# Input projections by seven products of quarters, all ahead of the attention, with their results kept in DRAM

## The chip, the cores and the metric

The kernel runs on one core of a Trainium2 chip. The metric is the device time of one launch in microseconds. TensorE (PE) multiplies, VectorE (DVE), ScalarE (ACT) and GpSimd (POOL) do the elementwise work, and SyncE (SP) issues nearly all DMAs, one after the other in the order of its queue.

## The reference

One step of a hybrid decoder layer. 560 tokens (16 meta, 512 prompt, 32 sample tokens of 8 sequences) of width 1024 go through an RMS norm, and one wide projection feeds two branches:

```python
hn = rmsnorm(x, norm_g)
proj = jnp.einsum('btd,dn->btn', hn, w_in)
a_pool, z_pool, q, k, v, o, z_m, i_pre, f_pre, g_pool, g_mlstm = split_projection(proj)
y_pool = multiscale_pool(pool_buf, a_pool, ...) * silu(z_pool)      # trailing means, then a map per group
(C_new, n_new, m_new), h = mlstm_scan(q, k, v, ig, lf, state, ...)   # 4 heads of 512, matrix memory
y_mlstm = sigmoid(o) * layernorm_per_head(h) * silu(z_m)
u = sigmoid(g_pool) * (y_pool @ w_branch_pool) + sigmoid(g_mlstm) * (y_mlstm @ w_branch_mlstm)
y = rmsnorm(x + u @ w_out, final_g)
```

a_pool, z_pool, g_pool and g_mlstm are 1024 wide, q, k, v, o and z_m 2048 each. Besides y the outputs are the new states, among them the matrix memory of 8 sequences and 4 heads (512 x 512 each), which is read, scaled, added to and written.

## The kernel before

All products keep float32 accuracy with three passes: each operand is split into a high and a low part (`split`, L105: ACT casts the high part, DVE or POOL subtracts), and `mm3` (L123, its matmul is L129) multiplies low by high, high by low and high by high, for each of the 8 slabs of 128 inputs. The normed input lies in SBUF transposed, as `hT_hi` and `hT_lo` of 128 x 8 x 560.

A projection (`project`, L131) takes 128 columns of `w_in`: `weights` (L114) loads 512 KB in one DMA, ACT casts `whi`, DVE subtracts `wlo`, and 2 x 24 matmuls of 272 or 280 token columns fill two PSUM banks, which ACT or DVE read at once. V is made the other way round, with tokens on the partitions (L607, 512 columns).

The program is written in one order and a scheduler keeps dependences; each engine runs its own list strictly in that order. `begin` (L187) makes `hT` and the first two projections (L77); `gates` (L338) makes the rows of input and forget gates on 4 partitions and writes them to DRAM as `rows_d` (L407); `pooling` (L437) holds the projections of the pooling branch, and its work and the gates' run side by side. Then come four `head`s (L579 on): V, then q and k, then the state products `prompt_C` (L709) and `sample_C` (L726 to L736), the scores, and o and z_m of the head between them, the numerators and the layer norm. In a head the projections stand between the steps that wait for DVE and ACT. `final` (L955 on) does the branch products, `w_out` and the last norm. Weights are loaded some units ahead: `wraw`, `whi` and `wlo` share 12 buffers of 4 KB a partition. At a head's start `bc`, the head's gate rows on all partitions, is loaded from `rows_d` (L584).

What each head needs of the projections is used where it is made: q, k, v, o and z_m never leave SBUF or PSUM.

## Time and profile before

| what | value |
|---|---|
| median of 3 runs | 1133.23 us (1133.14 to 1138.13) |
| span of the profiled execution | 1129.6 us |
| PE, DVE, ACT, POOL busy | 98%, 54%, 33%, 19% of the span |
| bytes moved by DMA | 177.18 MB, 157 GB/s |
| granted TensorE clock, mean | 0.997 |

The profile shows one execution and gives its span, from the first to the last instruction; its own time, with what lies around the span, is not listed, and the timed runs' median stands 3.6 us above the span. A matmul's shown duration overlaps the next one's, so a matmul's cost is read from the spacing in the chain and not from its own mean.

### The profile page before, as it was taken

The numbers are of one execution on the slowest core, as the hardware profiler recorded it, in microseconds if no ns is written. First come the engines' busy times: TensorE is split into PE (matmuls) and PEld (weight loads), VectorE is DVE, ScalarE is ACT, GpSimd is POOL, SyncE is SP. The second block draws the span as 40 slices with busy tenths as digits, with TensorE's granted clock in tenths as the row PEclk, the third lists the DMA queues.
The fourth block names the chain that finished last, engine by engine and source line by source line (L and its number), as shares of the span: only waits on it lengthen the run. The fifth ranks groups of instructions, "written<-read, shape, count | busy, mean of one in ns | idle before, by whom it ended". The sixth has DMA issues, their size and how long they took to land.

```text
span 1129.6 us, 19419 instructions
## 1 busy us (share of the span) xinstructions
PE 1112.0 (98%) x7938; PEld 1016.7 (90%) x7938; DVE 613.9 (54%) x954; ACT 373.6 (33%) x688; POOL 218.8 (19%) x367
## 2 busy tenths in 40 slices
PE   7999999999999999999999999999999989999997
PEld 6999999989879889979889979889978889999976
DVE  6786732224545755446655456556447465265633
ACT  5642342113222343232342232343222334342322
POOL 4223220003205003205003215003214001020000
PEclk9999999999999999999999999999999999999999
DMA  8432433434566744566654566754565754343512
GB/s 210 128 110 73 111 86 107 126 97 113 178 204 211 231 143 135 176 203 221 222 164 124 173 193 204 232 176 118 167 223 192 237 179 133 107 132 118 180 52 84
DMA packets 188176, 177.18 MB, mean 157 GB/s; under 512 B 12479, under 2 KB 137167, under 8 KB 187563
## 3 DMA queue, kind: packets, MB, share of 16 engines
q1 hardware_dynamic: 188087, 175.94, 50.9%
q8 instruction: 62, 1.02, 0.4%
q14 instruction: 27, 0.22, 0.1%
HBM read 127.80 MB, written 47.39 MB: 155 GB/s over the span
## 4 chain that ended last, share of the span: by engine, by line
PE 77%; DMA 9%; DVE 8%; issue 2%; ACT 1%; SPq 1%; POOL 0%; DVEq 0%; POOLq 0%; ACTq 0%
PE ps L129 57%; PE ps L607 8%; DMA wraw<-in_w_in_dram 6%; DVE C L733 3%; PE ps L709 3%; PE ps L726 2%; PE ps L795 1%; DMA out_dram<-C 1%; PE ps L609 1%; ACT whi L108 1%; DVE wlo L111 1%; DVE vc L767 1%; DMA x<-in_x_prompt_dram 1%; PE ps L695 1%; PE ps L732 1%
## 5 line engine op out<-in xcount | busy, mean ns | idle before, releaser
L129 PE MATMUL ps<-hT_hi,wlo 128*128 128x272 f32 (+1 forms) x1504 | 439.5, 292 | 0.3 <-DVE yp L493 0.3
L129 PE MATMUL ps<-hT_hi,whi 128*128 128x272 f32 (+1 forms) x1504 | 435.3, 289 | 0.0
L129 PE MATMUL ps<-hT_lo,whi 128*128 128x272 f32 (+1 forms) x1504 | 435.1, 289 | 0.0
L111 DVE TENSOR_TENSOR wlo<-wraw,whi 128x1024 fp32r<-128x1024 f32 x134 | 168.0, 1254 | 338.3 <-ACT whi L108 227.0
L129 PEld LDWEIGHTS ps<-hT_hi,wlo 128*128 128x128 f32 x1504 | 284.2, 189 | 15.1 <-issue 10.4
L129 PEld LDWEIGHTS ps<-hT_hi,whi 128*128 128x128 f32 x1504 | 284.7, 189 | 0.0
L129 PEld LDWEIGHTS ps<-hT_lo,whi 128*128 128x128 f32 x1504 | 283.8, 189 | 0.2
L108 ACT CAST whi<-wraw 128x1024 fp32r<-128x1024 f32 x134 | 140.6, 1049 | 393.7 <-DMA wraw<-in_w_in_dram 313.6
L733 DVE SCALAR_TENSOR_TENSOR C<-C,bc,ps 128x512 f32<-128x512 f32 x128 | 87.4, 739 | 6.6 <-PE ps L732 6.6
L129 PE MATMUL ps<-yh,whi 128*128 128x272 f32 x256 | 72.9, 288 | 0.0
L129 PE MATMUL ps<-yl,whi 128*128 128x272 f32 x256 | 72.8, 288 | 0.0
L129 PE MATMUL ps<-yh,wlo 128*128 128x272 f32 x256 | 70.5, 289 | 0.0
L111 POOL TENSOR_TENSOR vl<-v,vh 128x512 fp32r<-128x512 f32 x16 | 31.8, 2023 | 110.3 <-issue 84.5
L607 PE MATMUL ps<-whi,hT_lo 128*128 128x512 f32 x128 | 50.5, 395 | 0.0
L607 PE MATMUL ps<-whi,hT_hi 128*128 128x512 f32 x128 | 50.4, 393 | 0.0
L607 PE MATMUL ps<-wlo,hT_hi 128*128 128x512 f32 x128 | 50.2, 393 | 0.0
L129 PEld LDWEIGHTS ps<-yh,whi 128*128 128x128 f32 x256 | 48.2, 188 | 0.0
L129 PEld LDWEIGHTS ps<-yl,whi 128*128 128x128 f32 x256 | 48.2, 188 | 0.0
L129 PEld LDWEIGHTS ps<-yh,wlo 128*128 128x128 f32 x256 | 46.9, 188 | 0.0
L726 PE MATMUL ps<-C,qm 128*32 128x512 f32 x256 | 40.7, 603 | 0.0
L111 POOL TENSOR_TENSOR kl<-k,kh 128x560 fp32r<-128x560 f32 x16 | 22.3, 1396 | 90.2 <-DVE r_hi L673 77.3
L129 PE MATMUL ps<-ypl,whi 128*128 128x272 f32 x128 | 36.9, 288 | 0.0
(315 smaller groups left out, 1806.7 us busy)
## 6 DMA issues: line engine op xcount, KB each, us to landing
wraw<-in_w_in_dram SPq DMA_DIRECT2D x112, 512.0 KB
C<-in_state_C_dram SPq DMA_DIRECT2D x64, 512.0 KB
out_dram<-C SPq DMA_DIRECT2D x64, 512.0 KB
wraw<-in_w_branch_mlstm_dram SPq DMA_DIRECT2D x16, 512.0 KB
bc<-rows_d SPq DMA_DIRECT2D x4, 1256.0 KB
wraw<-in_w_branch_pool_dram SPq DMA_DIRECT2D x8, 512.0 KB
out_dram<-c SPq DMA_DIRECT2D x16, 256.0 KB
wraw<-in_w_out_dram SPq DMA_DIRECT2D x8, 512.0 KB
```

Of the source, the lines that this page charges most:

```text
L108: nc.scalar.copy(hi, src)
L111: (lo_on or nc.gpsimd).tensor_tensor(lo, src, hi.bitcast(F32), ALU.subtract)
L129: self.nc.tensor.matmul(out, s, m, start=(j == 0), stop=(j == len(seq) - 1))
L607: nc.tensor.matmul(pv[i], s, w[:, k2], start=(k == 0 and j == 0), stop=(k == 7 and j == 2))
L609: nc.tensor.matmul(pv[4][:112], self.hS[:, k], w[:, k2], start=(k == 0 and j == 0), stop=(k == 7 and j == 1))
L695: nc.tensor.transpose(ps[:, i * P:(i + 1) * P], kw[:, i * P:(i + 1) * P], self.ident)
L709: nc.tensor.matmul(pc, s[:, i], m[:, i], start=(i == 0 and j == 0), stop=False)
L726: nc.tensor.matmul(pqc[r:r + 32], self.qm[:, d, 32 * b:32 * b + 32], Cs[bb // 2][:, bb % 2], start=(d == 0 and g == 0), stop=(d == 3 and g ...
L732: nc.tensor.matmul(pu, kwst[r:r + 12, g], vst[r:r + 12, g], start=True, stop=True, tile_position=(r, 0))
L733: V.scalar_tensor_tensor(C, C, wintb[:, b, 3:4], pu, ALU.mult, ALU.add)
L767: V.scalar_tensor_tensor(t[:n], vh[:n, i].bitcast(F32), vs[:n, i:i + 1], vl[:n, i].bitcast(F32), ALU.subtract, ALU.add)
L795: nc.tensor.matmul(pb[:, o:o + mv.shape[-1] - m], s, mv[:, m:], start=(j == 0), stop=(j == last[True]))
```

## The change

Two column tiles of 128 are now made together (`quad`, L171 of the new file). The 1024 inputs are cut in two halves of 4 slabs, the 256 columns in two of 128, the 560 tokens in two of 280, and the eight products of quarters are replaced by seven, on sums and differences of quarters. Sums of the input, `Sa` to `Sd`, are made once in `begin`; sums of the weights are made in each `quad`. Three results are kept by ACT (`keep`), and DVE makes three of the four output quarters from them (`total`). A `quad` has 84 matmuls where two `project`s had 96. V and the first two tiles of the pooling input stay as they were. There are 47 quads, 36 of 272 columns and 11 of 280.

The token columns are in another order (`COLS`), so that the two halves are alike. All projections come first (`projections`), head by head, with the pooling branch and the sample states between the o and z_m quads; q, k, v, the gates' product `og`, the pooling branch's `yp` and `sg` and the samples' `qc` go to DRAM. `attention` then reads them back, head by head. `rows_d` is now written in eight pieces, and V's first part reads two small pieces of it back (`sw`).

Three places show the new order. The first is SP's queue after the gate rows. `rows_d` is the gates' DRAM scratch, `wraw` a projection's weights, `bc` and `sw` gate rows on all partitions. Before:

```order
L410 DMA out_dram<-gm_524 4x8x1
L115 DMA wraw_1207<-in_w_in_dram 128x8x128
L407 DMA rows_d<-rw 4x2512
L115 DMA wraw_1268<-in_w_in_dram 128x8x128
L584 DMA bc_2640<-rows_d 128x2512
L115 DMA wraw_1347<-in_w_in_dram 128x8x128
L586 DMA bc_2640<-in_c_sel_dram 32x48
L115 DMA wraw_1474<-in_w_in_dram 128x8x128
```

and now, where `wraw_598` holds the first weights of V of head 0:

```order
L545 DMA rows_d<-em_498 4x544
L545 DMA rows_d<-wi_497 4x32
L545 DMA rows_d<-ws_496 4x560
L751 DMA sw_595<-rows_d 128x32
L752 DMA sw_595<-rows_d 128x32
L751 DMA sw_2708<-rows_d 128x32
L754 DMA wraw_598<-in_w_in_dram 128x2x512
L752 DMA sw_2708<-rows_d 128x32
L754 DMA wraw_632<-in_w_in_dram 128x2x512
```

The load of the first weights after the gates now stands behind the eight pieces of `rows_d` and behind a read of them, where before one weight load stood right in front of the write and the others around it.

The second is PE in a projection, with the PSUM bank first (`ps_...`). Before, where the second half of the tokens follows the first:

```order
L129 MATMUL ps_826<-hT_hi,wlo_823 128x272
L129 MATMUL ps_826<-hT_lo,whi_822 128x272
L129 MATMUL ps_826<-hT_hi,whi_822 128x272
L129 MATMUL ps_851<-hT_hi,wlo_823 128x272
L129 MATMUL ps_851<-hT_lo,whi_822 128x272
L129 MATMUL ps_851<-hT_hi,whi_822 128x272
```

and now, at the end of a q quad of head 0 (`Sc` is one of the input's sums, `wblo` and `wbhi` weights' sums):

```order
L146 MATMUL ps_814<-Sc_hi,wblo_811 128x272
L146 MATMUL ps_814<-Sc_lo,wbhi_810 128x272
L146 MATMUL ps_814<-Sc_hi,wbhi_810 128x272
L146 MATMUL ps_814<-hT_hi,wblo_811 128x272
L146 MATMUL ps_814<-hT_lo,wbhi_810 128x272
L146 MATMUL ps_814<-hT_hi,wbhi_810 128x272
```

Before, the next product goes to another bank; now the last product of the quad adds to the bank that DVE has to read between the two.

The third is SP's queue at the start of a head. `vpt` takes copies of the head's v parts, made by ACT and POOL or DVE. Before, in head 0:

```order
L629 DMA vs_d_2889<-vh_2643 48x512 x2
L629 DMA vs_d_2889<-vl_2644 48x512
L636 DMA vpt<-vh_2643 16x512
L636 DMA vpt<-vl_2644 16x512
L632 DMA vst_2646<-vs_d_2889 12x1x512 x8
L636 DMA vpt<-vh_2643 16x512
L115 DMA wraw_3279<-in_w_in_dram 128x8x128
L722 DMA C_3377<-in_state_C_dram 128x2x512
```

and now in head 1, where `k_1682`, `k_1694`, `k_1710` are the first three slabs of k, `q_...` slabs of q and `og` the head before's gated outputs:

```order
L1030 DMA k_1682_9601<-k_d 128x560
L1102 DMA v_1681_9593<-qc_d 32x512
L1010 DMA vpt<-vh_9568 16x512 x2
L1010 DMA vpt<-vl_9569 16x512
L1103 DMA v_1681_9593<-v_1681_9593 48x512
L1023 DMA q_1691_9636<-q_d 128x544
L1030 DMA k_1694_9642<-k_d 128x560
L1023 DMA q_1703_9667<-q_d 128x544
L1030 DMA k_1710_9708<-k_d 128x560
L1064 DMA out_dram<-c_1709_9705 128x512
L1183 DMA y_d<-og_9281 128x544
```

Before, weights and states stood behind the copies into `vpt`; now the slabs of q and k of the same head do, and its last ones stand behind the stores of the head before.

The diff, cut to what the new order and the new product consist of:

```diff
...
+    def quad(self, src, lo, dst, scale=None, f21=None):
+        nc = self.nc
+        V, A = nc.vector, nc.scalar
+        n = HN - lo
+
+        def wide(n, pair):
+            return self.c(n, F32R, (2, 4, P)) if pair else self.c(n, F32R, (4, 256))
+
+        def narrow(n):
+            return self.r(n, F32R)[:, :512].rearrange("p (k n) -> p k n", k=4)
+        ra, rb = (self.c(s, shape=(4, 256)) for s in ("wa", "wb"))
+        nc.sync.dma_start(ra, src[:, 0:4])
+        nc.sync.dma_start(rb, src[:, 4:8])
+        b11, b12, b21, b22 = ra[:, :, :P], ra[:, :, P:], rb[:, :, :P], rb[:, :, P:]
+        ta, tb = (self.c(s, shape=(2, 4, P)) for s in ("ta", "tb"))
+        w11 = self.parts(b11, lambda s: narrow("w1" + s))
+        V.tensor_tensor(ta[:, 0], b11, b12, ALU.add)
+        V.tensor_tensor(ta[:, 1], ta[:, 0], b22, ALU.add)
+        wa = self.parts(ta, lambda s: wide("wa" + s, True))
+        V.tensor_tensor(tb[:, 0], b12, b22, ALU.add)
+        V.tensor_tensor(tb[:, 1], ta[:, 1], b21, ALU.add)
+        w2 = self.parts(rb, lambda s: wide("w2" + s, False))
+        wb = self.parts(tb, lambda s: wide("wb" + s, True))
+        hT, S = self.hT, self.S
+
+        def quarter(half, kh):
+            return [tuple(t[:, 4 * kh + k, HN * half + lo:HN * half + HN] for t in hT) for k in range(4)]
+
+        def combined(s):
+            return [tuple(t[:, k, lo:] for t in S[s]) for k in range(4)]
+
+        def product(ps, w, movs, first):
+            self.mm3(ps[:, :n], [(w[0][:, k], w[1][:, k]) for k in range(4)], movs, first=first, check=False)
+
+        def at(w, j):
+            return tuple(t[:, j] for t in w)
+
+        def cols(w, j):
+            return tuple(t[:, :, j * P:(j + 1) * P] for t in w)
+
+        def keep(ps, name):
+            t = self.t(name)[:, :n]
+            A.activation(t, ps[:, :n], AF.Copy, scale=1.0 if scale is None else scale)
+            return t
+
+        def view(ap, c0, c1, how):
+            ap = ap[:, c0:c1]
+            return how(ap) if how else ap
+
+
+        def total(which, ps, other, s_ps, s_other):
+            for out, c0, c1, how in dst[which]:
+                x, y = view(ps, c0, c1, how), view(other, c0, c1, how)
+                if scale is not None:
+                    V.scalar_tensor_tensor(out, x, s_ps * scale, y, ALU.mult, ALU.add if s_other > 0 else ALU.subtract)
+                elif s_ps < 0:
+                    V.tensor_tensor(out, y, x, ALU.subtract)
+                else:
+                    V.tensor_tensor(out, x, y, ALU.add if s_other > 0 else ALU.subtract)
+
+        pa, pe = self.ps(), self.ps()
+        product(pa, w11, quarter(0, 0), True)
+        p1 = keep(pa, "p1")
+        product(pe, at(wa, 0), combined("a"), True)
+        e = keep(pe, "e")
+        product(pa, at(wa, 1), combined("b"), False)
+        u = keep(pa, "u")
+        product(pe, cols(w2, 1), combined("d"), False)
+        total("12", pe, u, 1, -1)
+        px = self.ps()
+        product(px, cols(w2, 0), quarter(0, 1), True)
+        total("11", px, p1, 1, 1)
+        product(pa, at(wb, 0), combined("c"), False)
+        total("22", pa, e, -1, 1)
+        product(pa, at(wb, 1), quarter(1, 1), False)
+        for out, c0, c1, how in dst["21"]:
+            A.activation(out, view(pa, c0, c1, how), f21 or AF.Copy, scale=1.0 if scale is None else scale)
+
+
...
+            self.v_d = scratch("v_d", H, NT, HD + 1)
+            self.qc_d = scratch("qc_d", H, 32, HD)
+            with reused("combined", side="right") as self.sp, reused("hidden") as self.ip:
+                self.S = {s: [self.sp.tile([P, 4, HN], F32R, name=f"S{s}_{p}") for p in ("hi", "lo")] for s in "abcd"}
+                with reused("begin") as self.wp:
+                    self.begin()
+                with reused("work") as self.wp:
+                    self.projections()
+            with reused("branch", side="right") as self.bp:
+                with reused("heads") as self.hp:
+                    self.attention()
+            with reused("final") as self.fp:
                 self.final()
...
+
+        x = {}
+        for half in range(2):
+            for kh in range(2):
+                x[half, kh] = self.wp.tile([P, 4, HN], F32, name=f"x{half}{kh}")
+                hi, lo = (t[:, 4 * kh:4 * kh + 4, HN * half:HN * half + HN].bitcast(F32) for t in self.hT)
+                G.tensor_tensor(x[half, kh], hi, lo, ALU.add)
+        a, b, c, d = x[1, 1], x[0, 0], x[1, 0], x[0, 1]
+        V.tensor_tensor(a, x[1, 0], a, ALU.subtract)
+        V.tensor_tensor(c, x[0, 0], c, ALU.subtract)
+        V.tensor_tensor(b, a, b, ALU.subtract)
+        V.tensor_tensor(d, d, b, ALU.add)
+        for s, t in ("a", a), ("b", b), ("d", d), ("c", c):
+            self.split(*self.S[s], t, A, V)
...
+        nc.scalar.activation(emr, m[:, 16:], AF.Exp, scale=-2.0)
+        V.tensor_scalar(emr, emr, 1.0e37, None, ALU.min)
+        for i, t in [*zip(SEGO, sv), (OEM, emr), (OWI, wir), (OWS, wsr)]:
+            nc.sync.dma_start(self.rows_d[:, i:i + t.shape[-1]], t)
...
+    def projections(self):
+        a = self.gates()
+        self.pool_begin()
...
+        for h in range(H):
+            for part in self.unit_v(h):
+                do(part, 0.6)
+            if h == 0:
+                self.gate_columns(a)
+            for j in range(2):
+                do(lambda: self.unit_q(h, j), 1.0)
+            while later:
+                later.pop(0)()
+            for j in range(2):
+                self.unit_k(h, j)
+            rest = [lambda j=j, f=f: f(h, j) for j in range(2) for f in (self.unit_o, self.unit_zm)]
+            mine, fill = fill[:share[h]], fill[share[h]:]
+            units = []
+            while rest or mine:
+                units += rest[:1] + mine[:1]
+                rest, mine = rest[1:], mine[1:]
+            later = [lambda h=h, j=j: self.sample_C(h, j) for j in range(8)] + [lambda h=h: self.sample_q(h)]
+            self.pace = (len(units) + (4.4 if h < 3 else 0)) / 9.5
+            credit = self.pace
+            for u in units:
+                do(u, 1.0)
+        while later:
+            later.pop(0)()
+        self.sample_end()
+
...
+        def part(kk):
+            if kk == 0:
+                pv.extend(self.ps() for _ in range(5))
+                sw = self.sw[h] = self.wp.tile([P, 2, 32], F32, tag="sw", name=f"sw{h}", bufs=2)
+                nc.sync.dma_start(sw[:, 0], self.rows_d[h, OWI:OWI + 32].partition_broadcast(P))
+                nc.sync.dma_start(sw[:, 1], self.rows_d[h, OWS + 528:OWS + 560].partition_broadcast(P))
+            raw = self.c("wraw", shape=(2, HD))
+            nc.sync.dma_start(raw, self.w_in[:, 2 * kk:2 * kk + 2, CV + h * HD:CV + (h + 1) * HD])
+            wh, wl = self.parts(raw, lambda s: self.c("w" + s, F32R, (2, HD)))
+            for k2 in range(2):
...
+            if d:
+                G.tensor_tensor(self.qns[:, h], self.qns[:, h], qn, ALU.add)
+            nc.sync.dma_start(self.q_d[:, 4 * h + d], q[n][:, :NO])
...
+        def load_rows():
+            nc.sync.dma_start(bc, self.rows_d[h].partition_broadcast(P))
+
+            nc.sync.dma_start(bc[48:80, SEGO[4]:SEGO[4] + 48], I["c_sel"])
+
+        def load_v():
+            for i in range(5):
+                n = TILEN[i]
+                t = self.r("v32")
+                nc.sync.dma_start(t[:n, :HD + 1], self.v_d[h, TILE0[i]:TILE0[i] + n])
+                v32.append(t)
+                m = n if i < 4 else 16
+                self.split(vh[:m, i], vl[:m, i], t[:m, :HD], A)
+                G.tensor_scalar(vs[:n, i:i + 1], t[:n, HD:HD + 1], -1.0 / HD, None, ALU.mult)
+
...
+                nc.sync.dma_start(self.vpt[32 * j:32 * j + 16].bitcast(F32), t[:16, 4].bitcast(F32))
...
+        def load_q(d):
+            t = self.r("q32")[:, :NO]
+            nc.sync.dma_start(t, self.q_d[:, 4 * h + d])
+            qh, ql = self.r("qh", F32R, rb=True), self.r("ql", F32R, rb=True)
+            self.split(qh[:, 16:], ql[:, 16:], t, A, V)
             qT.append((qh, ql))
 
...
+        def load_k(d):
             k32 = self.r("k32")
...
+            nc.sync.dma_start(k32, self.k_d[:, 4 * h + d])
             kw = self.r("kw")
             V.tensor_tensor(kw, k32, wsb, ALU.mult)
...
+        load_rows()
+        load_v()
+        for d in range(4):
+            load_k(d)
+            if d == 0:
+                decays()
+            k_rows(d)
+            load_q(d)
+            if d == 1 and self.late:
+                self.late()
+            if d:
+                prompt_C(d - 1)
+        prompt_C(3)
         scores()
         key_sums()
-        sample_C(3)
-        unit_z(0)
-        prompt_C(3)
-        sample_C(4)
         for i in range(4):
-            centre_v(i, self.r("vc")[:, :HD])
-        unit_o(1)
-        unit_z(1)
-        sample_C(5)
-        unit_o(2)
+            centre_v(i)
+        centre_tail()
+        load_og()
+        for u in fill:
+            u()
         denominators()
-        sample_C(6)
-        unit_z(2)
-        unit_o(3)
-        sample_C(7)
-        sample_q()
-        unit_z(3)
-        if h == 3:
-            for m in range(self.Y0):
-                self.y_load(m)
         s = numerators()
         sh, sl_ = self.r("sh", F32R)[:, :NO], self.r("sl", F32R)[:, :NO]
         self.split(sh, sl_, s, None, V)
         self.late = lambda: variances(sh, sl_)
...
```

## Rows read from the trace of the kernel before

**Rows 1.** The page: span, and section 1 (engine, busy us, share, instructions).

```profile
span 1129.6 us, 19419 instructions
...
PE 1112.0 (98%) x7938; PEld 1016.7 (90%) x7938; DVE 613.9 (54%) x954; ACT 373.6 (33%) x688; POOL 218.8 (19%) x367
```

**Rows 2.** The page, section 4: shares of the chain by engine and line.

```profile
PE ps L129 57%; PE ps L607 8%; DMA wraw<-in_w_in_dram 6%; DVE C L733 3%; PE ps L709 3%; PE ps L726 2%; PE ps L795 1%; DMA out_dram<-C 1%; PE ps L609 1%; ACT whi L108 1%; DVE wlo L111 1%; DVE vc L767 1%; DMA x<-in_x_prompt_dram 1%; PE ps L69
```

**Rows 3.** Busy time of each engine by stretch: one head.

```profile
core 0: us, PE busy (x) PEld busy (x) DVE busy (x) ACT busy (x) POOL busy (x), PEclk, DMA share, GB/s
...
405.00:576.00 171.00, 171.00 (x1199) 151.22 (x1198) 97.44 (x152) 54.68 (x103) 36.32 (x73) 1.00 0.59 185
```

**Rows 4.** Chain of waits, 225 to 410 us.

```profile
259.09 36.46 PE ps L129 x288
...
302.35 2.76 PE ps L709 x12
...
361.67 4.82 DMA wraw<-in_w_in_dram
```

**Rows 5.** Chain of waits in order of time, 0 to 80 us (start, us, what).

```profile
22.49 2.67 DVE hT_lo L77 x5
...
25.20 6.79 PE ps L77 x47
...
38.24 4.12 PE ps L352 x32
42.36 12.18 PE ps L129 x96
```

**Rows 6.** Groups of POOL (count, busy us, mean ns, idle before and releaser).

```profile
L111 POOL TENSOR_TENSOR vl<-v,vh 128x512 fp32r<-128x512 f32 x16 | 31.8, 2023 | 110.3 <-issue 84.5 <-DVE vh L110 25.8
...
L77 POOL TENSOR_TENSOR wlo<-wraw,whi 128x1024 fp32r<-128x1024 f32 x2 | 5.0, 2492 | 1.1 <-ACT whi L77 1.1
```

**Rows 7.** Timeline 24 to 46 us, POOL (start, us, engine, line, what).

```profile
26.97 1.70 POOL L111 TENSOR_TENSOR wg<-wg_raw,wg 128x512 fp32r<-128x512 f32 x1 [0.52 <-ACT wg L108]
```

**Rows 8.** Timeline 42 to 77 us, DVE: the first gate row.

```profile
42.28 0.50 DVE L356 SCALAR_TENSOR_TENSOR ig<-ps,gbi,ig 4x280 f32<-4x280 f32 x1 [0.31 <-ACT zf L355]
```

**Rows 9.** Timeline 42 to 77 us, ACT: the last gate row.

```profile
75.42 0.70 ACT L404 ACTIVATE rw<-rw 4x592 f32<-4x592 f32 x1 [1.96 <-DVE rw L401]
```

**Rows 10.** Groups of DVE between 42.2 and 76.2 us: rows that are not the gates.

```profile
L111 DVE TENSOR_TENSOR wlo<-wraw,whi 128x1024 fp32r<-128x1024 f32 x6 | 7.3, 1213 | 0.8 <-ACT whi L108 0.8
...
L460 DVE TENSOR_TENSOR S<-E 128x679 f32<-128x679 f32 x2 | 1.7, 838 | 0.0
L460 DVE TENSOR_TENSOR S<-S 128x664 f32<-128x664 f32 x2 | 1.7, 832 | 0.0
```

**Rows 11.** Timeline 42 to 86 us, SP's queue.

```profile
76.15 0.25 SPq L407 DMA_DIRECT2D rows_d<-rw  x1
...
78.87 0.35 SPq L584 DMA_DIRECT2D bc<-rows_d  x1
...
84.69 0.33 SPq L586 DMA_DIRECT2D bc<-in_c_sel_dram  x1
```

**Rows 12.** Groups of DVE.

```profile
L111 DVE TENSOR_TENSOR wlo<-wraw,whi 128x1024 fp32r<-128x1024 f32 x134 | 168.0, 1254 | 338.3 <-ACT whi L108 227.0 <-PE ps L129 67.3 <-PE ps L609 42.5
L733 DVE SCALAR_TENSOR_TENSOR C<-C,bc,ps 128x512 f32<-128x512 f32 x128 | 87.4, 739 | 6.6 <-PE ps L732 6.6
...
L871 DVE RECIPROCAL D<-D 128x544 f32<-128x544 f32 x4 | 14.2, 3554 | 3.4 <-ACT D L870 3.4
...
L836 DVE TENSOR_TENSOR sz<-ps,sz 128x272 f32<-128x272 f32 x32 | 14.0, 437 | 15.0 <-ACT sz L835 15.0
...
L873 DVE TENSOR_TENSOR og<-og,D 128x544 f32<-128x544 f32 x16 | 12.8, 863 | 0.1
...
L668 DVE TENSOR_TENSOR kw<-k,bc 128x560 f32<-128x560 f32 x16 | 11.8, 739 | 17.6 <-ACT k L666 17.6
...
L111 DVE TENSOR_TENSOR kwl<-ps,kwh 128x512 fp32r<-128x512 f32 x16 | 10.9, 681 | 0.0
```

928 lines of the change are left out of this document (495 added, 433 removed).

## The prediction

> **What bounds the kernel now.** I read the page first: PE is busy 98% of a span of 1129.6 us, DVE 54%, ACT 33%, POOL 19% [rows 1]. The shares of the chain by line say the same in another way: more than half of the span is the three-pass projection matmul of L129, 8% the V projection, and only 6% is the landing of weights [rows 2]. The busy time by stretch shows whether that is an average over good and bad parts: in a whole head, 171 us, PE is busy 171.00, although the scores, the gates and the layer norm of that head wait for DVE, ACT and DMA [rows 3]. So the projections do two things: they are the bulk of the work, and they are the cover for everything that is slow. The granted clock in that stretch is 1.00, the upper level of 2.4 GHz. A kernel that is bound by PE gains what it takes off PE, as long as nothing else then waits; it loses every gap that the order opens. There is almost no idle time to win back, so the change must pay for its gaps out of the matmuls it saves.
>
> **What it removes.** 47 quads have 84 matmuls in place of 96, so 47 x 12 = 564 go. In the chain 288 matmuls of 272 columns take 36.46 us [rows 4], 0.1266 each, and the 32 of 280 columns 4.12 us [rows 5], 0.129 each. 36 x 12 x 0.1266 + 11 x 12 x 0.129 = 54.7 + 17.0 = 71.7 us. This is the firmest number here, since the instruction list shows the matmuls gone and their size is unchanged. If the weight loads of another stationary part were slower it could shrink a little; I keep it.
>
> **The start.** Before, hT's last low part is there at 22.49 + 2.67 = 25.2 us, PE goes on to 42.4 us through the last L77 products and the gates, and from then on it has projections of the pooling branch [rows 5]. Now the gates and V of head 0 are all there is. Step by step: POOL makes three sums of 1120 elements ahead of the gate weights' low part. A POOL row of 1024 of this kind takes 2.49 us [rows 6], so 2.73 each, 8.2 in all, to 33.4 us; the gate weights' row takes 1.70 [rows 7], to 35.1; the gate products 4.1, to 39.2. Then PE has a few transposes and stands before V. The gate rows ran before from 42.28 to 75.42 + 0.70 = 76.1, that is 33.8 us [rows 8, 9]. In that time DVE also did weight splits of 7.3 us and pooling rows, whose two largest groups are 1.7 each [rows 10], together with smaller ones 13 to 15. Without them the gates take some 20. Now five of the eight rows on the input's sums, 1.37 each by the split's 1.254 for 1024 [rows 12], stand among them: 27 to 28, so the gates end at about 67. Then SP's queue: before, `rows_d` is written at 76.15 and the read that waits for it goes out at 78.87, so a write lands in 2.7 us [rows 11]. Now eight writes, that wait, then `sw`, and only then V's first weights, issued at about 71. A 512 KB weight load has taken 4.82 us in the chain [rows 4], and its high part is needed before PE can begin: 77 us. PE stands from 39.2 to 77, 37.8 us, and from the end of the first products at 25.2 + 6.8 = 32.0 [rows 5] to 35.1, 3.1 us, less its transposes: 40 us. Before, the same queue waited as long, but PE had weights in hand, so it cost nothing. Low end 25, if the gates go without DVE's rows in between; high end 50, if DVE takes the sums first.
>
> **Between the products of a quad.** The fourth output quarter is read by DVE from the bank to which the seventh product then adds. The read is 0.437 us for 272 columns [rows 12]. In the new instruction list the seventh product follows the sixth directly in 19 of 47 quads, has some four to eight matmuls of another bank between them in 11, and more in the rest. DVE's queue is strict, and the row ahead of the read is often a split of 1.254 us [rows 12]; with half of it in the way and the handover, I take 1.0 for the 19 and 0.45 for the 11: 24 us. It can be 0 if DVE always stands ready and other products cover it, and 47 x (0.437 + 1.254) = 79 if it always has just begun a split; I stay near the read's own row.
> The Trainium skill, page "Perfetto Trace Analysis", section "Matmuls", says that groups of matmuls should rotate through PSUM banks, so that the read of one lies beside the next one's matmuls. By it alone, all 47 quads would pay, 47 us in place of 24, 23 later; the list shows that the next quad's first products stand between in 17 of them, and the kernel before, which rotates, has no such wait.
>
> **DVE and SP in the projections.** Per quad DVE has five rows of 512 (0.681), three splits of 1.254 and three totals of 0.437, 8.5 us [rows 12], where two projections had two splits, 2.5. PE needs 84 x 0.1266 = 10.6. With the samples' 32 rows of 0.739 per head, a head's projections are by this count 164 to 180 us on PE and 139 to 174 on DVE. So DVE has room on the whole and not locally: in heads 0 and 1 the rows bunch after K and run about 20 us behind, of which two quads' buffers hide most. I take 4. At the change from V to Q and K, SP's queue holds the stores of V ahead of the next weights; I take 2 per head, 8. Together 12, between 0 and 45, the latter if neither is hidden.
>
> **The start of the attention.** `bc` lies where hT was, so its load can go only after the last quad. Before, the load issued at 78.87 was followed by a dependent one at 84.69, so it lands in 5.8 us [rows 11]. Mask, k times its row (0.74 for 560 elements, by the 0.739 of a like row) and transposes follow, and all that PE has hangs on it: 12 us, between 7 and 20.
>
> **The heads.** Let N be the end of a head's numerators. The next head's v parts lie in the same single buffers, so only then ACT casts and POOL subtracts, at 2.023 us a row of 512 [rows 6]: four rows, N + 8.5. The copies into `vpt` wait for that, and behind them in SP's queue stand the second slab of k and its q. It lands at about N + 13.5, and PE's order has the second slab's transposes ahead of the first state product, so this starts at N + 15. Then DVE has the reciprocal, 3.554, and four rows of 0.863 [rows 12] ahead of the third slab, 7 us, and SP has the stores of these four ahead of the fourth. The last state product ends at N + 33 to 38. PE's work until there is 4 x 2.76 [rows 4] and small things, 15. So a head waits 18 to 23 where before projections stood in the gaps; with loads somewhat earlier than that I take 15 for each of three heads, and 5 in head 0, where the pooling branch's inputs come late: 50. From 0, if k and v are prefetched after all, to 3 x 23 + 8 = 77.
>
> **The end** starts on loads that wait for the heads' memory: 4, between 0 and 8.
>
> **The sum.** -71.7 + 40 + 24 + 12 + 12 + 50 + 4 = +70.3 on the profiled execution's span of 1129.6, which is 1199.9; the median lies 3.6 above the span, so 1203.5 us.
>
> **Rivals.** First, faster: the waits are covered. In the projections buffers of two quads absorb the reads and DVE's bunches, and in the heads SP's queue runs ahead, so only the start's 40 and some 12 stay: 1129.6 - 71.7 + 52 + 3.6 = 1113.5; with the low end of the start 25 and nothing else 1086.5, and with no wait at all 1061.5. For it speaks that PE was at 98% in a program with as many dependences; against it, that the cover in those heads was the projections themselves, which now lie elsewhere. It decides from the point at which all added waits together are below 71.7 us. Second, DVE becomes the bound of the projections: its strict queue has a split waiting for its weights or a total for its product, and cannot use the room it has. By the count above its rows in the projections come to 614 us. If it loses a tenth of that, 61 us, of which 12 stand in the sum, the time is 1252. DVE's 54% now and the many waits of its own speak against so much. Third, about no change: the gates, the reads and half of the heads' waits come as worked out, but the rest is hidden: 71.7 against 70 to 75.
>
> **How the numbers follow.** The forecast has a chance of 0.60, with its own range of 1155 to 1245; DVE as the bound 0.10, faster 0.23, no change 0.07. A measurement of this kernel tells about 0.5% (5.7 us) from no change. Slower by more: 0.70; within: 0.07; faster: 0.23. The range of 1100 to 1250 leaves out the deeper half of the faster case (0.11) and about 0.07 above.
>
> **What would show it.** PE idle between about 39 and 77 us, ended by the weights' landing: right for the start; a first V matmul before 60 us would break that step. A wait of PE for DVE's total in about 20 quads, 20 to 30 us in the list of waits; below 10 the bank is covered. In the heads, PE idle after each numerator for 10 us or more, then a second gap after DVE's reciprocal. PE's busy time should be near 1040 us. If the heads take below 50 us each, or PE's idle time is below 70 in all, the forecast is wrong and the faster case holds.

## The result and the profile after

The changed kernel takes 1605.1 us, the median of 4 runs (1603.9 to 1608.6), beside 1135.7 us for the kernel before on the same chip. The ratio is 1.414, 95% interval 1.409 to 1.419. Slower was right; the size was not: 1203.5 us was forecast, with a range that ended at 1250.

First the page of the changed kernel: span, busy times, the clock by fortieths of the span, the chain's largest shares.

```profile
span 1606.8 us, 19729 instructions
...
PE 1182.9 (74%) x7390; PEld 1047.4 (65%) x7390; DVE 861.2 (54%) x1365; ACT 548.5 (34%) x1013; POOL 174.3 (11%) x338
...
PEclk9588898878888888799899899988776879699999
...
PE 53%; DVE 17%; DMA 13%; ACT 7%; issue 5%; POOL 3%; SPq 1%; DVEq 0%; ACTq 0%; POOLq 0%
```

PE was busy 1112.0 us of 1129.6 before [rows 1]. Now it has 548 recorded products fewer and is busy 71 us longer, with 424 us of idle time where it had 18. So two things went wrong, and they can be added up against the forecast, which had 1040.3 us of busy time and 159.6 of idle time: 143 us are more busy time for the products, 264 us are more waits. The same trace by four stages shows where (bounds: V's first product, the last product on the input, the first product of the last stage).

```profile
core 0: us, PE busy (x) PEld busy (x) DVE busy (x) ACT busy (x) POOL busy (x), PEclk, DMA share, GB/s
0.00:81.40 81.40, 31.97 (x179) 26.43 (x179) 48.63 (x93) 30.94 (x64) 23.46 (x31) 0.76 0.33 65
81.40:1105.70 1024.30, 784.76 (x4930) 688.44 (x4930) 568.11 (x903) 338.43 (x591) 27.78 (x138) 0.87 0.47 152
1105.70:1442.40 336.70, 212.40 (x1266) 189.97 (x1264) 163.53 (x233) 129.71 (x268) 105.95 (x142) 0.79 0.43 141
1442.40:1606.80 164.40, 153.74 (x1020) 142.60 (x1020) 80.89 (x138) 49.37 (x92) 17.10 (x27) 0.97 0.34 109
```

PE idles 49 us at the start, 240 in the projections, 124 in the heads and 11 at the end. Before, a whole head with its projections had PE busy in every microsecond at a granted clock of 1.00 [rows 3]; no stage has that now. The list of PE's waits (us in total, times, longest) names them (`kw` is a slab of k times its gate row, `kst` the samples' masked copies of k):

```profile
PE ps L146 <- DVE w1lo L120: 131.0, 29, 18.1
PE ps L1047 <- DVE kw L1032: 96.8, 11, 11.3
PE ps L726 <- DMA n_raw<-in_state_n_dram: 32.5, 1, 32.5
PE ps L858 <- POOL kst L850: 21.7, 8, 5.4
PE ps L762 <- ACT whi L117: 20.1, 3, 8.5
PE ps L146 <- DVE q L222: 18.0, 4, 7.5
PE ps L146 <- DVE k L220: 16.0, 8, 2.8
```

The first line was in no step of the prediction. `w1` is the split of the first weight quarter of a quad, the stationary part of its first product. One place on DVE's timeline (start, us, what, and in brackets the idle time before) shows why it is late; rows of three quads stand in it:

```profile
410.52 1.22 DVE L120 TENSOR_TENSOR walo<-ta,wahi 128x1024 fp32r<-128x1024 f32 x1 [6.44 <-PE ps L146]
...
414.69 0.68 DVE L120 TENSOR_TENSOR w1lo<-wa,w1hi 128x512 fp32r<-128x512 f32 x1
...
420.94 0.69 DVE L182 TENSOR_TENSOR ta<-wa 128x512 f32<-128x512 f32 x1 [4.08 <-DMA wa<-in_w_in_dram]
...
424.83 1.23 DVE L120 TENSOR_TENSOR walo<-ta,wahi 128x1024 fp32r<-128x1024 f32 x1 [1.12 <-PE ps L146]
...
427.87 1.22 DVE L120 TENSOR_TENSOR w2lo<-wb,w2hi 128x1024 fp32r<-128x1024 f32 x1
429.00 0.69 DVE L120 TENSOR_TENSOR w1lo<-wa,w1hi 128x512 fp32r<-128x512 f32 x1
```

PE, from 426 to 431 us:

```profile
426.63 0.29 PE L146 MATMUL ps<-Sc_hi,wbhi 128*128 128x272 f32 x1
429.75 0.40 PE L146 MATMUL ps<-hT_hi,w1lo 128*128 128x280 f32 x1 [2.83 <-DVE w1lo L120]
...
430.64 0.30 PE L146 MATMUL ps<-hT_hi,w1lo 128*128 128x280 f32 x1
430.77 0.41 PE L146 MATMUL ps<-hT_lo,w1hi 128*128 128x280 f32 x1
430.97 0.43 PE L146 MATMUL ps<-hT_hi,w1hi 128*128 128x280 f32 x1
431.20 0.43 PE L146 MATMUL ps<-hT_hi,w1lo 128*128 128x280 f32 x1
```

SP's queue:

```profile
415.41 0.40 SPq L177 DMA_DIRECT2D wa<-in_w_in_dram  x1
...
429.72 0.38 SPq L177 DMA_DIRECT2D wa<-in_w_in_dram  x1
```

By the buffer numbers of the instruction list, the `w1lo` at 429.00 belongs to a quad A whose own `walo` ran at 410.52, 19 rows earlier. The `ta`, `walo` and `w2lo` from 420.94 to 427.87 are those of the next quad, B. They wait 4.1 us for B's load, so A's first product, at 429.75, waits for B's load too. That load went out at 415.41, 0.04 us after the `w1lo` of the quad before A had ended (414.69 + 0.68), and the `wa` of the quad after B goes out at 429.72, 0.03 us after A's: `w1lo` is the last reader of a `wa` buffer. So in this place the load of one quad, its sums and splits, and the first product of the quad before it follow each other, 14.3 us a round where 84 products need 10.6. In 36 of the 46 quads that have a next one, `w1lo` stands behind the next quad's first sum; in 6 of the 47 a `wa` goes out within 0.1 us after the end of such a `w1lo`, and elsewhere other waits of SP's queue come last. The instruction list also has the row last among its own quad's: later in the program, between a quad's `walo` and its `w1lo` on DVE, there are 24 other rows.

```
702 L120 TENSOR_TENSOR walo_6435<-ta_6426,wahi_6434 128x1024
...
715 L120 TENSOR_TENSOR wblo_6445<-tb_6427,wbhi_6444 128x1024
...
727 L120 TENSOR_TENSOR w1lo_6429<-wa_6422,w1hi_6428 128x512
```

The PE rows also show the slower products: spaced 0.13 us up to 430.77, then 0.20 and 0.23 us. By stretch:

```profile
424.00:430.70 6.70, 3.52 (x26) 3.09 (x25) 5.87 (x9) 3.59 (x5) 0.00 (x0) 1.00 0.00 0
430.70:434.00 3.30, 3.30 (x16) 3.30 (x15) 0.47 (x1) 0.40 (x1) 0.00 (x0) 0.51 0.93 259
```

After a stretch with PE busy for 3.5 us of 6.7, the granted clock drops from 1.00 to 0.51, from the level of 2.4 GHz to that of 1.2, and the following products cost nearly double although they wait for nothing. The Trainium skill, page "TensorE: Matmul & The Clock Gate", section "HAM oscillation — how this bites in real kernels", describes a kernel whose gaps between groups of products throw the clock back each time; this trace agrees in kind, with the drop above and 0.87 as the mean in the projections. Summed over all stretches of the trace at the lower level (granted clock 0.50), PE is busy 242 us in them. At 0.23 us in place of 0.13 between products, some 105 of these are what the lower level costs, by this estimate the larger part of the 143 us; where the rest comes from is not shown.

### The profile page after: what moved, and what is told of

Same layout as the page of the kernel before. It is cut to its first block, busy times and chain, and to the rows that moved or that the text cites. A ratio compares the mean times of both kernels' runs of the same rounds, so it can differ in the third digit from the quotient of the medians.

```text
span 1606.8 us, 19729 instructions
## 1 busy us (share of the span) xinstructions
PE 1182.9 (74%) x7390; PEld 1047.4 (65%) x7390; DVE 861.2 (54%) x1365; ACT 548.5 (34%) x1013; POOL 174.3 (11%) x338
## 4 chain that ended last, share of the span: by engine, by line
PE 53%; DVE 17%; DMA 13%; ACT 7%; issue 5%; POOL 3%; SPq 1%; DVEq 0%; ACTq 0%; POOLq 0%
PE ps L146 39%; PE ps L762 6%; DMA wb<-in_w_in_dram 3%; PE ps L1060 3%; DVE C L887 2%; DMA bc<-rows_d 1%; DVE w1lo L120 1%; DMA vs_d<-vsl 1%; DVE w2lo L120 1%; POOL vl L120 1%; DMA wpraw<-in_w_pool_dram 1%; DMA C<-in_state_C_dram 1%; PE ps L880 1%; PE ps L764 1%; ACT wahi L117 1%
## 5 line engine op out<-in xcount | busy, mean ns | idle before, releaser
L146 PE MATMUL ps<-hT_hi,w1lo 128*128 128x272 f32 (+1 forms) x188 | 73.1, 389 | 131.1 <-DVE w1lo L120 131.0
L120 DVE TENSOR_TENSOR wlo<-wraw,whi 128x1024 fp32r<-128x1024 f32 x40 | 50.3, 1257 | 107.5 <-ACT whi L117 55.3
L887 DVE SCALAR_TENSOR_TENSOR C<-C,sw,ps 128x512 f32<-128x512 f32 x128 | 88.9, 742 | 22.7 <-PE ps L886 18.1
L146 PE MATMUL ps<-yy,whi 128*128 128x272 f32 x512 | 97.8, 294 | 4.1 <-DVE yy L120 4.1
L146 PEld LDWEIGHTS ps<-yy,whi 128*128 128x128 f32 x512 | 82.0, 194 | 4.3 <-DVE yy L120 4.3
L146 PE MATMUL ps<-yy,wlo 128*128 128x272 f32 x256 | 74.1, 297 | 3.7 <-ACT yy L117 3.7
L1047 PEld LDWEIGHTS ps<-ident,kw 128*128 128x128 f32 x64 | 10.6, 196 | 100.4 <-issue 74.1
L146 PE MATMUL ps<-hT_hi,w1hi 128*128 128x272 f32 (+1 forms) x188 | 68.1, 362 | 0.0
L146 PE MATMUL ps<-hT_lo,w1hi 128*128 128x272 f32 (+1 forms) x188 | 68.0, 362 | 0.0
L146 PE MATMUL ps<-Sa_hi,walo 128*128 128x272 f32 (+1 forms) x188 | 65.1, 346 | 0.0
L146 PE MATMUL ps<-Sa_lo,wahi 128*128 128x272 f32 (+1 forms) x188 | 63.8, 339 | 0.0
```

What stands on the lines that cost most here:

```text
L120: (lo_on or nc.gpsimd).tensor_tensor(lo, src, hi.bitcast(F32), ALU.subtract)
L146: self.nc.tensor.matmul(out, s, m, start=(first and j == 0), stop=(j == len(seq) - 1), skip_group_check=not check)
L887: V.scalar_tensor_tensor(C, C, wintb[:, b, 3:4], pu, ALU.mult, ALU.add)
L1047: nc.tensor.transpose(ps[:, i * P:(i + 1) * P], kw[:, i * P:(i + 1) * P], self.ident)
```

## Experiments

Each edit is on the kernel named; unless a ratio stands there, the time is of one execution, and the kernel before took 1130.9 to 1135.5 us beside it. Every edit lets the order of all instructions be made anew, so I read differences under some 15 us as none. The stages are those of the four rows above (length in us):

| run | us | start | projections | heads | end |
|---|---|---|---|---|---|
| changed kernel | 1605.1 | 81.4 | 1024.3 | 336.7 | 164.4 |
| c_on_pool | 1623.1 | 81.0 | 1044.1 | 331.8 | 164.4 |
| small_18 | 1589.4 | 80.9 | 1013.7 | 328.3 | 164.6 |
| w1_in_large | 1447.9 | 81.1 | 866.8 | 333.9 | 164.3 |
| w1_own | 1443.1 | 81.6 | 854.5 | 345.7 | 159.5 |
| plain_pairs | 1404.6 | 80.0 | 821.4 | 336.9 | 164.5 |
| plain_shallow | 1431.4 | 79.5 | 838.6 | 333.8 | 177.6 |
| start_first | 1448.1 | 80.3 | 865.9 | 335.5 | 164.7 |
| rows_apart | 1443.9 | 81.2 | 865.9 | 330.5 | 164.5 |
| bank_and_queues | 1457.2 | 80.7 | 869.3 | 340.8 | 164.6 |
| four_edits | 1445.2 | 80.1 | 868.8 | 330.9 | 163.6 |
| deep_buffers | 1445.1 | 84.5 | 856.4 | 337.8 | 164.6 |
| w2lo_on_pool | 1460.5 | 80.5 | 878.6 | 335.2 | 164.5 |
| start_and_k | 1396.1 | 45.3 | 845.2 | 339.7 | 164.1 |
| plain_start_and_k | 1386.7 | 46.5 | 835.4 | 338.4 | 164.6 |
| weights_by_pool | 1374.2 | 56.9 | 825.1 | 325.8 | 164.6 |
| plain_by_pool | 1380.9 | 55.7 | 818.0 | 340.4 | 165.0 |
| no_C_update | 1336.9 | 45.2 | 787.5 | 337.8 | 164.6 |
| late_first | 1370.3 | 56.7 | 823.3 | 327.1 | 163.8 |

**The late w1.** Four runs on the changed kernel. My theories were: A, that w1 comes late because it waits for one of the small buffers it takes, and holds `wa`; B, that SP's queue is blocked by the stores of C that wait for DVE (SP waits 246 us for them in the changed kernel); C, that DVE's 8.5 us of rows a quad set the pace.

```diff
# c_on_pool: sample_C
-            nc.sync.dma_start(C, I["state_C"]...)      (and the store)
+            nc.gpsimd.dma_start(C, I["state_C"]...)
# w1_in_large: quad
-        w11 = self.parts(b11, lambda s: narrow("w1" + s))
+        w1 = self.c("w1", F32R, (2, 4, P))
+        w11 = self.parts(b11, lambda s: w1[:, 0 if s == "hi" else 1])
# small_18
-    RS, CS, RB = 16, 18, 13
+    RS, CS, RB = 18, 18, 11              # and bufs=4 in place of 5 for the kept products
# plain_pairs: quad makes the four quarters as two plain projections, 96 products
```

> The changed kernel with the loads and stores of the samples' states C issued from POOL's queue in place of SP's, nothing else. Theory B (SP's queue: the stores of C wait for DVE, 246 us in all, and hold the next quads' weights behind them): 150 us or more faster, below 1455. Theory A (the small 560-word buffers: the first quarter's split weights come last of a quad's preparation, since they wait for a buffer, and keep the raw weights' 4-KB buffer, so that the next load is late): within 40 of 1605. Theory C (DVE's own work of 8.5 us per quad): within 30.

> The changed kernel with the two split parts of the first quarter in one 4-KB buffer in place of two 560-word buffers, nothing else. Theory A: 100 us or more faster, with the wait of PE for DVE's w1lo (131 us) mostly gone. Theory B and theory C: within 40 of 1605, since SP's queue and DVE's work are the same; with 11 large buffers a quad in place of 10 it could also be a little slower if the large buffers are what is short.

> The changed kernel with 18 in place of 16 of the 560-word buffers (paid with one of the five buffers for kept products and two of the attention's 13). Theory A: 50 to 150 us faster in the projections. Theories B and C: within 30 of 1605.

> The changed kernel with each quad made as two plain projections of 24 matmuls a half (96 in place of 84), in the same order and with the same DRAM copies; three of four outputs are still copied by DVE. Theory A and theory C both say that it is faster although PE has 72 us more: A, since no small buffers and 6 of 18 large ones are held in place of 10, below 1350; C, since DVE's work per pair falls from 8.5 to 3.8 us, below 1400. Theory B: slower by up to 70, since the stores of C hold the weights as before.

B fell: with C on POOL's queue the time rose by 18 us. A's price held: one large buffer for w1's two parts took 157 us away, all in the projections, and C fell with it, since DVE's rows are the same. A's reason did not hold: two more small buffers took only 16 where I had 50 to 150, PE still waits 126.5 us for `w1lo`, and the row still stands behind the next quad's first sum in 36 of 46 quads. So the number of small buffers was not it, and why the order gave the row that place stays open. Plain pairs are faster still by 43, so here the form costs more than it saves; they miss A's 1350 and, by 5, C's 1400. What w1_in_large left open is whether w1 gained by leaving the shared buffers or by having several at once:

```diff
# w1_own
-    RS, CS, RB = 16, 18, 13
+    RS, CS, RB = 16, 17, 13
+        w1 = self.mp.tile([P, 2, 4, P], F32R, tag="w1", name=self.name("w1"), bufs=1)
```

> Like the changed kernel, but w1's two parts have one 4-KB buffer of their own, and there is one large buffer less (17), so that neither the number nor the size of the buffers grows. Theory (w1 came last because the shared small buffers it took are held by long-lived tiles, and so it got a late place in DVE's fixed order, behind the rows of other work): it comes out near w1_in_large, 1448 us, within 25, and PE's wait for w1's low part falls from 131 us below 50. Rival (w1_in_large gained by the deeper buffers: a second quad's w1 prepared while the first is still in use): with one buffer the next w1 waits for the third product of the quad before, and the time stays above 1520.

It was the first: a single buffer of its own, with one large buffer less, gives 1443.1 us. PE's waits in w1_own (`w` is w1 here):

```profile
PE ps L1048 <- DVE kw L1033: 99.7, 12, 11.4
PE ps L859 <- POOL kst L851: 35.7, 8, 6.7
PE ps L727 <- DMA n_raw<-in_state_n_dram: 32.0, 1, 32.0
PE ps L146 <- DVE w L120: 21.1, 2, 13.9
```

131 us have become 21. Of the other waits some moved: those for q's totals (18 us) are gone, those for `kst` rose from 22 to 36. On DVE w1's low part now follows directly on the first sum of its quad in 24 of 47 quads, as here, and stands behind a sum of the next quad in none:

```profile
361.68 0.69 DVE L183 TENSOR_TENSOR ta<-wa 128x512 f32<-128x512 f32 x1 [2.02 <-DMA wa<-in_w_in_dram]
362.39 0.69 DVE L120 TENSOR_TENSOR w<-wa,w 128x512 fp32r<-128x512 f32 x1
```

From the issue of a quad's `wa` to the end of its `w1lo` the median is 10 us, where the changed kernel has 31.

**The bank, the start, the rows of a head.** Four runs on w1_in_large.

```diff
# start_first: projections (prep = load and split, without the products)
+        parts0 = self.unit_v(0)          # prep of three parts of V
+        self.pool_begin(); self.unit_a(0, self.first)
         a = self.gates()
# rows_apart: head
-        bc = hp.tile([P, ROWN], ...)
+        bc, em2, wsb = three tiles, loaded apart
# bank_and_queues: quad; vpt, y_d and C_prompt on nc.gpsimd
         product(pa, at(wb, 0), combined("c"), False)
         total("22", pa, e, -1, 1)
+        px = self.ps()
+        product(px, cols(w2, 0), quarter(0, 1), True)
+        total("11", px, p1, 1, 1)
         product(pa, at(wb, 1), quarter(1, 1), False)
```

> Like w1_in_large, but the first three loads and splits of head 0's V weights, and the copies of the first projection out of its banks, stand ahead of the gates; the two rows that V does not need are read behind them. Theory (what is late at the start is the place of V's weights behind the gates on DVE and SP): first V matmul at about 40 us in place of 81, the fourth part of V still waits for a row that stands behind the gates, so the time falls by 30 to 40 us, from 1448 to about 1412. Rival (the projections are bound by their own waits, so an earlier start is only stood out later): V starts at 40, but the time falls by less than 10.

> Like w1_in_large, but the broadcast rows of a head lie in three tiles (decays, key weights, denominator's bound) in place of one, so that the next head's decays and key weights can be loaded while the numerators run. Theory (a head's chain begins with the rows, 6.4 to 8.3 us of landing and 5 of exponentials behind the denominators of the head before): the attention falls from 334 us by 10 to 13 in each of three heads, to about 300. Rival (v's parts on POOL, which wait for the numerators, and the copies behind them on SP come last anyway): it falls by less than 10 in all.

> Like w1_in_large with two edits in different stages. In a quad the product for the 11 quarter, which has a bank of its own, is moved between the read of the 22 quarter and the seventh product. In the heads the copies into the tail of v and the stores of y and of C go by POOL's queue in place of SP's. Theory of the bank: PE's waits for the totals, 14.4 us in w1_in_large, fall below 5, and the projections from 867 us by 10 to 20 with the clock; rival: another wait takes their place, within 5. Theory of the heads (k's loads stand behind those copies in SP's queue, 2.2 and 2.8 us of the chain and what waits on them): the attention falls from 334 by 5 to 10 a head, to about 305; rival (k's splits stand behind v's on ACT and DVE too): within 8.

> Like w1_in_large with the edits of start_first, rows_apart and bank_and_queues together. If each stage has its own cause the gains add: start -40, projections -10 to -20 less what V's fourth part gives back (10), attention -50: 1448 to about 1350. If one chain carries the next (rival), the time stays above 1390. In either case it stays above the 1131 to 1136 of before, since the gaps in the projections that come from the preparation of the weights are not touched.

None of the four moved the time by more than 10 us, and three theories of mine fell with them. The start: V's first product stayed at 80.3 us, since PE's order has the transposes of the state's n rows ahead of V, and these waited 32.6 us for their load. The rows of a head: 3 us. The bank: PE's waits for totals (the lines with q, k, zm, zx, sg, so and E) are 49 us in 23 places in the changed kernel, but 14 in w1_in_large with the same banks, and with a product between they are 13: most of them came with the late w1, not with the bank.

**What paces the projections.** Three runs on w1_in_large and one on plain_pairs.

```diff
# start_and_k: start_first, and
+        self.sample_begin()              # n rows ahead of V's parts
-            for j in range(2):
-                self.unit_k(h, j)
+            ks = [self.unit_k(h, j) for j in range(2)]   # kst and its transposes one quad later
# deep_buffers: input sums left out, their 36 KB as nine buffers for wa, wb, ta, tb
# plain_shallow: plain_pairs
-    RS, CS, RB = 16, 18, 13
+    RS, CS, RB = 16, 10, 13              # and bufs=2 for vh, vl, bc
# w2lo_on_pool: quad
-        w2 = self.parts(rb, lambda s: wide("w2" + s, False))
+        w2 = self.parts(rb, lambda s: wide("w2" + s, False), nc.gpsimd)
```

> Like start_first with two more edits. The state's n rows, for which PE stood 32.6 us in start_first because their load goes out behind the gates' writes in SP's queue, are loaded and transposed ahead of the gates. And the sample part of k (masked copies on POOL, transposes on PE) comes one quad later, so that PE's order no longer has these transposes right behind k's last product; PE's wait for them was 37 to 39 us in eight places. Theory (PE's fixed order has one instruction ahead whose input comes late, and all behind it waits): V's first product at about 40 us in place of 81, the wait for the copies below 10, and the time falls by 40 to 70 us, from 1448 to 1380 to 1405. Rival (the projections are paced by the preparation of the weights, and stand the gain out at the next quad): below 20 in all.

> Like w1_in_large, but the sums of the input's quarters are left out (the products read plain quarters of the input in their place), and the 36 KB so freed serve as nine more large buffers, for a quad's two loads and its two pairs of weight sums. A quad takes eleven large buffers, so eighteen hold 1.6 quads, where a pair of plain projections takes six and eighteen hold three. Theory of the depth (weights of the next quad cannot be loaded and prepared while the present one runs): DVE's waits for the loads, 53 us in w1_in_large, nearly go, and the projections fall from 867 us to about 780 (705 of products and 50 to 75 of the waits that plain_pairs has too). Rival (DVE's fixed order with 8.5 us of rows a quad is the limit, whatever the buffers): they stay above 840. The start loses some 8 us of rows on POOL and DVE in either case.

> Like plain_pairs, but with 10 large buffers in place of 18 (1.7 pairs, as a quad has 1.6), and the 32 KB so freed give the heads two buffers each for v's two parts and for the rows of a head. Theory of the depth: the projections rise from 821 us to 870 to 900; rival: within 20 of 821. Theory of the heads (single buffers of v and of the rows make a head's chain begin only behind the numerators of the head before): the attention falls from 337 us to 260 to 280, PE's wait for k's weighted rows from 99 us below 40; rival (the order in the queues of SP, ACT and DVE is the limit): it stays above 315.

> Like w1_in_large, but the low part of w2 is subtracted on POOL in place of DVE, 47 rows of 1.25 us off DVE, at some 2.5 us each on POOL, which is idle there. Theory of DVE's load (8.5 us of rows a quad plus the samples' in a strict queue against 10.6 on PE): the projections fall from 867 us by 30 to 60. Theory of the depth (buffers, not DVE, set the pace): within 10, since a slower low part holds its buffers longer; it may even lose.

start_and_k gained 52 us, 36 of them at the start: with the n rows early, V's first product is at 45.3. PE's waits for `kst` are gone from its list. The other theories fell. Nine more large buffers gave 10 us in the projections; ten in place of eighteen cost plain pairs 17 there; with 47 rows less on DVE the time is 13 longer. And two buffers each for v and the rows of a head gave 3 us in the heads: PE's wait for `kw` fell from 99 to 75 us, and other waits took its place.

**What the form and the queues are worth when w1, the start and k are mended.**

```diff
# weights_by_pool: start_and_k, quad and V
-        nc.sync.dma_start(ra, src[:, 0:4])
+        nc.gpsimd.dma_start(ra, src[:, 0:4])        # rb and V's raw likewise
# and in head: k's and q's first slab loaded ahead of v's copies, c_sel behind prompt_C(3)
# no_C_update: start_and_k without pu, C's rows and stores; heads as above, and v's copies on nc.gpsimd
# plain_start_and_k: start_and_k with quad as in plain_pairs
# plain_by_pool: that, with the loads on nc.gpsimd and the heads of no_C_update
```

> Like start_and_k with two edits in different stages. The weights' loads of the quads and of V go by POOL's queue in place of SP's, where they stand behind stores that wait for DVE (241 us of waiting for C's update alone). In the heads the first slab of k and q is loaded ahead of v's copies, and the small selection rows, for which SP waited until the broadcast rows had landed (6 us), come behind the state products. Theory of SP's order: the projections fall from 845 us by 40 or more; rival (ACT's and DVE's own fixed order, or POOL's queue, which now waits in SP's place): within 15. Theory of the heads (SP's order): the attention falls from 340 us by 20 or more; rival (the chain of v's parts on POOL, its tail's copy and k's later slabs): within 10.

> Like start_and_k, but the samples' state C is read for the queries and not updated and not stored: 256 products of 512 columns, 256 rows of DVE of 0.74 us and 64 stores are left out. In the heads the edits of weights_by_pool, and v's copies into the tail by POOL's queue. If the samples' updates in the queues of SP and DVE pace the projections, they fall from 845 us by much more than the 256 products themselves (some 50 to 60 us of PE): to 740 or less. If not, by 60 at most, to about 785. In the heads: below 320 us if SP's copies behind v's parts hold back k, within 10 of 340 if not.

> Like start_and_k, but a quad is made as two plain projections of 96 products in all (as in plain_pairs), so that it differs from start_and_k by the seven-product form alone, with the late w1 already gone. plain_pairs was 43 us faster than w1_in_large. If the form itself costs by DVE's rows between the loads and the products, this stays some 40 us faster than start_and_k: about 1355. If the waits of start and of k were what made the form look dear, the two come within 15 of each other.

> Like plain_start_and_k with the weights' loads by POOL's queue and the edits of the heads of no_C_update. If SP's order holds back the weights in the projections too, they fall by 20 or more against plain_start_and_k; if plain projections with three pairs of buffers already cover that, within 10. The heads as in no_C_update. It should stay above 1250 and so above the kernel before (1131 to 1136) either way, since the start's 40 us and most of the heads' waits are left.

With the weights on POOL's queue, start and projections together end 8.5 us earlier (882.0 in place of 890.5; the projections alone are 20 shorter, but V begins 12 later), and 8.2 with plain pairs: SP's order is not what paces them. Without the updates of C the projections are 58 us shorter, 39 of it PE's own time for the products left out (128, not the 256 of the text), so the samples' updates do not pace them either. What paces the projections once w1 comes early stays open: start_and_k has 115 us of idle time left there, and its longest waits in them are for w1, for `walo` and for the high part of V's weights, 28 to 30 us each. The seven products against plain pairs, all else equal, first start_and_k, then plain_start_and_k, projections only:

```profile
45.30:890.50 845.20, 730.32 (x4931) 644.36 (x4930) 581.45 (x954) 341.76 (x603) 39.21 (x144) 0.93 0.55 182
```

```profile
46.50:881.90 835.40, 768.16 (x5492) 697.76 (x5491) 397.80 (x677) 226.07 (x372) 37.88 (x144) 0.95 0.59 186
```

The form takes 38 us off PE's busy time, not the 72 of its products, in part since more of them run at the lower level (69 us of busy time in such stretches against 36), and gives 48 us back as idle time (115 against 67), for 184 us of rows on DVE and 116 on ACT that plain pairs don't have. It is worth nothing here, and plain_start_and_k is still 250 us above the kernel before with the same number of products. That is the price of the staging as a whole: the order, the copies in DRAM, and the input's sums, which this kernel still makes and does not read. The parts were not taken apart.

**The reciprocal in the heads**, on weights_by_pool:

```diff
# late_first: head
         load_rows()
+        if self.late:
+            self.late()
         load_v()
-            if d == 1 and self.late:
-                self.late()
```

> Like weights_by_pool, but the variances, the reciprocal and the four scaled outputs of the head before stand ahead of the head's k and v on PE, ACT and DVE, in place of between the second and the third slab of k. Theory (these 8 us of DVE lie in the chain from k to the state products): the attention falls from 326 us by 5 to 8 in each of three heads, to 302 to 311, and the time from 1374 to about 1353. Rival (the first slab of k now stands behind them, and the chain through v's tail and the second slab comes last in any case): within 6 of 326. Either way far above the kernel before.

The heads stayed within 2 us, so the rival holds. This is the fastest variant that does all the work, timed in three rounds: 1370.3 us, 1.209 times the kernel before (1.205 to 1.212). No version beats the kernel before.

## Why the prediction was wrong

**The removed products** came out as counted (plain_start_and_k, which has them again, records 564 more), but their price, 0.1266 us, held only at the upper level of the clock. The sum had no term for the clock, though it opened 142 us of gaps in a kernel that had 18. Of the 407 us that the span lies above the forecast, 143 are more busy time, some 105 of them by the estimate above the clock's.

**The start** was right in size, 81.4 us for V's first product against 77, and incomplete in cause. SP's queue, then PE:

```profile
65.61 2.19 SPq L545 DMA_DIRECT2D rows_d<-rw  x5
...
68.28 0.34 SPq L722 DMA_DIRECT2D n_raw<-in_state_n_dram  x1
...
76.23 0.42 SPq L754 DMA_DIRECT2D wraw<-in_w_in_dram  x1
```

```profile
74.66 0.61 PE L726 MATMUL ps<-ident,n_raw 32*128 32x32 f32 x4 [32.49 <-DMA n_raw<-in_state_n_dram]
81.36 2.07 PE L762 MATMUL ps<-whi,hT_lo 128*128 128x512 f32 x4 [5.50 <-ACT whi L117]
```

The gates ended at about 65, near the 67 worked out, and the writes and V's load followed, at 76.2 for 71. But PE stood first at the n rows, which I had passed over as "a few transposes"; start_first showed that mending V's weights alone moves nothing.

**Between the products** I had 24 us in about 20 quads; the places were right (23), the time was 49, and the cause was wrong, since the runs show the late w1 behind it. The Trainium skill's rule of rotating banks (page "Perfetto Trace Analysis", section "Matmuls"), taken at 1.0 us for each of the 47 quads, gave 47, near the measured sum, but the same banks wait 14 us in w1_in_large: the agreement was chance.

**DVE and SP in the projections** is the step that failed: "two quads' buffers hide most", 12 us between 0 and 45, against an idle time of some 190 beside the totals. I had counted DVE's rows per quad, 8.5 us against PE's 10.6, and concluded that there is room. There was: 568 us of rows in 1024, where my count had 614. What the count can't show is the place of a row in a fixed order. The list that I read for the bank also had w1's low part last among its quad's rows; I looked at which instructions were added and not at which is needed first. In 36 of 46 quads it stood behind the next quad's first sum, so that the start of a quad hung on the load of the next one. w1_own shows the price of that one row's place, with all that the order made anew moves with it: 162 us, in the traces (spans 1606.8 and 1441.3) 118 us less idle time of PE and 47 less busy time. The rival "DVE as the bound" named the strict queue, and priced it at a tenth of DVE's rows.

**The start of the attention** was 12 us; PE's first wait there is 11.3.

**The heads** were 50, from 0 to 77; with the attention's start taken off, the idle time is 113. The mechanism was right, the landing times were early. One head, whose numerators of the head before end at N = 1274.5, by stretches of 10 us:

```profile
1274.00:1284.00 10.00, 0.61 (x7) 0.51 (x5) 5.66 (x7) 8.41 (x16) 5.91 (x10) 0.66 0.51 157
1284.00:1294.00 10.00, 1.51 (x5) 0.87 (x5) 4.90 (x7) 1.70 (x6) 6.07 (x7) 0.50 0.16 44
1294.00:1304.00 10.00, 5.81 (x22) 4.65 (x22) 5.24 (x9) 4.19 (x8) 1.38 (x1) 0.64 0.22 57
1304.00:1314.00 10.00, 2.94 (x10) 2.49 (x11) 8.38 (x10) 3.17 (x8) 1.58 (x1) 0.70 0.64 223
```

SP's queue in it:

```profile
1274.41 0.33 SPq L997 DMA_DIRECT2D bc<-in_c_sel_dram  x1
1274.80 2.31 SPq L1003 DMA_DIRECT2D v<-v_d  x5
...
1288.78 0.51 SPq L1010 DMA_DIRECT2D vpt<-vl  x1
1290.38 0.51 SPq L1103 DMA_DIRECT2D v<-v  x1
...
1294.05 0.33 SPq L1030 DMA_DIRECT2D k<-k_d  x1
```

And PE:

```profile
1284.98 1.09 PE L1047 MATMUL ps<-ident,kw 128*128 128x128 f32 x4 [10.37 <-DVE kw L1032]
...
1297.87 1.09 PE L1047 MATMUL ps<-ident,kw 128*128 128x128 f32 x4 [11.30 <-DVE kw L1032]
...
1311.06 1.09 PE L1047 MATMUL ps<-ident,kw 128*128 128x128 f32 x4 [7.37 <-DVE kw L1032]
```

I had v's low parts at N + 8.5, they end at N + 14, since v itself is only loaded at N + 0.3, behind the selection rows that wait for the broadcast; the second slab of k is issued at N + 19.6 for a landing that I had at N + 13.5; the first state product starts at N + 25 for N + 15, the last ends at N + 51 for N + 33 to 38. So PE waits 29 us for the first three slabs of k, where I took 15 for a head. Which link is to blame stays open: the rows, the double buffers, the copies' queue and the reciprocal each gave 3 us or nothing, k's and q's first slab with the selection rows 14, just under what I read as a difference, which the copies by POOL's queue took back (337.8 and 340.4 us in no_C_update and plain_by_pool). The chain runs through four queues in turn, and by my reading each link taken out left the next at about the same time. A kernel with all of them taken out at once was not tried.

**The end**: 11 us of idle time for 4.

Of the signs named, the two gaps in each head and PE's gap up to about 77 us came, and the waits for totals in about 20 quads, with twice the time; a busy time near 1040 us did not.

## What to carry to other kernels

Where engines work through a fixed order, price an added step by the place of its last needed row in that order, not by the engine's share of busy time: look up, for the first product of a group, where each of its inputs stands on every engine, and which buffer waits for it. Here a small tile that took its buffers from a shared ring had a late place, behind rows of the next group, and a buffer of its own, 4 KB, was worth 162 us; that a shared ring does this in general is not shown. A kernel that is 98% busy on TensorE has its clock as part of that, so a gap costs more than its length; and taking the projections from between the heads, with the copies in DRAM that it needs, cost 250 us here, more than three times what the seven products could save.
